# Column sums of the first modulation in pairs of channel tiles, with slab loads and weight loads on two issuing engines

## The chip, the cores and the metric

The kernel runs on one core of a Trainium2 chip. The metric is the device time of one execution in microseconds (us). Its engines run side by side, each with its own instruction list: TensorE (PE in the profile; PEld is its loading of weights), VectorE (DVE), ScalarE (ACT), GpSimd (POOL) and SyncE (SP). SP computes nothing: it issues transfers (DMAs) from device memory to the core. ScalarE can issue transfers too, in between its arithmetic.

## The reference

One layer of a diffusion backbone over 128 context tokens and 256 latent tokens, D_MODEL = 2048. What matters here is its beginning, for each of the two kinds of token:

```python
mod = jax.nn.silu(cond) @ lw['w_ada'] + lw['b_ada']
sh1, sc1, ga1, sh2, sc2, ga2 = [m[:, None, :] for m in jnp.split(mod, N_MOD, axis=-1)]
h = rmsnorm(x, lw['norm_pre_mix']) * (1.0 + sc1) + sh1
...
proj = h @ lw['w_in']      # columns: q | k | v | output gate | two low-rank factors | Fourier groups
```

After that come gated linear attention in both directions, a Fourier branch, the merge through sigmoid gates, an output projection and a SwiGLU feed-forward layer. All is in f32.

## The kernel before

All 384 tokens are kept transposed: 2048 channels are 16 channel tiles of 128 partitions, tokens run along the free axis. A product with a large weight is made in three passes: weight and activation are each split into a high part and a rest (`whi`/`wlo`, `A_hi`/`A_lo`, the latter being `hT[0]` and `hT[1]`), and high x high, high x rest and rest x high are added up. The high part is a copy on ScalarE (a cast), the rest a subtraction on VectorE.

The change is in the first stage, the first 140 us or so: a loop `for kb in range(KT)` over the 16 channel tiles. Tile `kb` of the normalised, modulated input h is made while tile `kb - 1` is multiplied into v, q and the low-rank factors. In an ordinary tile TensorE does, in this order:

- `gemv(kb)` (line 398): shift and scale of the tile's 128 channels, that is sums over all 2048 rows of `w_ada`, as 16 matmuls (32 records) that write 32 rows each into four row groups of the PSUM tile `pgm`. The weight slab of a tile (`slab`, 2 MB, in two halves of 1 MB) streams as the moving operand;
- a product into `px` (line 433 for one of two columns of q, or line 440, the low-rank factors, four tiles at a time, in tiles 6, 10 and 14);
- `vprod`, one of three passes of v (line 415): six matmuls of 512 columns;
- two transposes (line 515) of `ev`, to which ScalarE has copied the sums (line 509), back into `pgm`;
- the next `px` product, the second pass of v, possibly a third `px` product, and the third pass of v.

Behind the transposes VectorE forms the four row groups' sum `pm` (523), the modulation `mods` (526, 530) and the tile `scr` (532); ScalarE casts it to `A_hi` (302), VectorE subtracts for `A_lo` (303). Each `px` product is added to its accumulator by VectorE (`flush`, line 428) before `px` is written again. The splits of this tile's weights for v (`raw`: cast in 227, rest in 228) and q (`xraw`: cast in 363, rest in 364) are made in `split_w`; the subtractions are put off to the end of the tile (`lag`), behind `A_lo`. Tiles 1 and 2 (`wait`) have their sums later than the others, since slabs come late at the start.

The order on TensorE, ScalarE, VectorE and GpSimd is that in which the program is written (`manual_schedule`). SP, too, issues in the order written: in tile `kb` the two halves of slab `kb + 1` (`load_slab`, line 343), then the 512 KB of v's weights (`load`, line 199) and the 128 KB of q's (`load_w`, line 350) for tile `kb + 1`; after tile 4's also five small loads (`load_later`, lines 381 to 385). A load waits until its buffer is free: there are two of `raw`, two of `xraw`, and five half slabs. Each transfer signals its end on one of eight semaphores, which are dealt out in turn.

The same function `load` feeds all later stages; there SP issues its transfers.

Of the kernel before, what the change touches and what calls it, by code (L numbers as in the profile page):

```python
# [11 lines left out]
F32 = mybir.dt.float32  # L12
# [8 lines left out]
P = 128  # L21
D = 2048
KT = D // P
# [73 lines left out]
def tile_step(ctx: ExitStack, tc: tile.TileContext, a, o):  # L97
    nc = tc.nc
    PE, ACT, DVE, POOL, SP = nc.tensor, nc.scalar, nc.vector, nc.gpsimd, nc.sync
# [9 lines left out]
    spad = const.tile([P, KT, 32], F32, name="spad")  # L109
# [5 lines left out]
    ident = const.tile([P, P], F32, name="ident")  # L115
# [37 lines left out]
    for h in range(2):  # L153
        for n in range(8):
            src = a["w_in"][16 + 4 * h : 20 + 4 * h, n // 4, :, 256 * (n % 4) : 256 * (n % 4) + 256]
# [34 lines left out]
    srcs = iter(enumerate(srcs))  # L190
    raws, ready = [], []

    def load(raw=None):
        n, src = next(srcs, (0, None))
        if src is not None:
            if raw is None:
                raw = wp.tile([P, G], F32, tag="raw", name="raw", bufs=2)
            dst = raw if len(src.shape) == 2 else raw.rearrange("p (n x) -> p n x", n=src.shape[1])
            SP.dma_start(dst, src)
            raws.append((raw, n in folded))  # L200

    fold_in = []
# [42 lines left out]
    def take():  # L245
        return ready.pop(0)
# [54 lines left out]
    def split_act(hi, lo, src):  # L301
        ACT.copy(hi, src)
        DVE.tensor_sub(lo, src, hi.bitcast(F32))
# [31 lines left out]
    with ExitStack() as s:  # L335
        pa = s.enter_context(tc.tile_pool(name="pa", bufs=1))
        pb = s.enter_context(tc.tile_pool(name="pb", bufs=2))
        slabs = {}

        def load_slab(kb):  # L340
            slabs[kb] = [pb.tile([P, KT // 2, 256], F32, tag="slab", name="slab", bufs=5) for _ in range(2)]
            for n, sl in enumerate(slabs[kb]):
                SP.dma_start(sl, a["w_ada1"][kb, :, n * (KT // 2) : (n + 1) * (KT // 2), :])

        xraw = {}

        def load_w(kb):
            load()
            xraw[kb] = pb.tile([P, XU * P], F32, tag="xraw", name="xraw", bufs=2)
            SP.dma_start(xraw[kb], a["w_x"][kb])  # L350

        def split_w(kb, defer):

            hi, lo = (wp.tile([P, G], F32R, tag=n, name=n, bufs=4) for n in ("whi", "wlo"))
            hi, lo = hi[:, 0 : XU * P], lo[:, 0 : XU * P]
            raw = xraw.pop(kb)

            if kb == 0:
                ACT.copy(hi, raw)
                defer.append(lambda: DVE.tensor_sub(lo, raw, hi.bitcast(F32)))  # L360
            split(defer=defer)
            if kb:
                ACT.copy(hi, raw)
                defer.append(lambda: DVE.tensor_sub(lo, raw, hi.bitcast(F32)))
            return take(), (hi, lo)

        xn, xnt = halves("C")
        for q in range(4):
            SP.dma_start(
                xnt[q // 2][:, 4 * (q % 2) : 4 * (q % 2) + 4, :], a["xT"][:, 4 * q : 4 * q + 4, :],  # L370
            )
        load_slab(0)
        SP.dma_start(cols, a["b_ada"])
        SP.dma_start(norms, a["norms"])
        load_w(0)
        load_slab(1)
        load_w(1)
        wlr = pa.tile([P, KT, 32], F32, name="wlr")

# [8 lines left out]
        pv = [psm.tile([P, 512], F32, tag="mm", name="pv") for _ in range(3)]  # L388
        pv += [pss.tile([P, 512], F32, tag="side", name="pv") for _ in range(3)]
        pgm = pss.tile([P, 512], F32, tag="side", name="pgm")  # L390
        pgv, pmod = pgm[:, 0:256], pgm[:, 256:512]
        px = pss.tile([P, T], F32, tag="side", name="px")

        def gemv(kb, ks=range(KT)):
            slab = slabs[kb]
            for k in ks:
                q = 32 * (k % 4)
                PE.matmul(  # L398
                    pgv[q : q + 32, :], spad[:, k, :], slab[k // (KT // 2)][:, k % (KT // 2), :],
                    start=k < 4, stop=k >= KT - 4,  # L400
                )

        def passes(w):
            return ((0, w[0]), (0, w[1]), (1, w[0]))

        def vprod(kb, w, parts, ts=range(3)):
            js = passes(w)
            tg = [(t, g) for t in ts for g in range(2)]
            if kb < KT - 1:
                order = [(j, t, g) for j in parts for t, g in tg]  # L410
            else:
                order = [(j, t, g) for t, g in tg for j in parts]
            for j, t, g in order:
                x_, w_ = js[j]
                PE.matmul(  # L415
                    pv[2 * t + g], hT[x_][:, kb, t * P : (t + 1) * P], w_[:, g * 512 : (g + 1) * 512],
                    start=kb == 0 and j == 0, stop=kb == KT - 1 and j == 2,
                )
# [46 lines left out]
        DVE.tensor_scalar_add(bsc1[:, 0, :], cols[:, 1, :], 1.0)  # L465
        DVE.tensor_scalar_add(bsc1[:, 1, :], cols[:, 4, :], 1.0)
        gemv(0, range(KT // 2, KT))
        ev = pb.tile([P, 256], F32, tag="ev", name="ev")
        ACT.copy(ev, pgv)
        for t in range(3):  # L470
            PE.matmul(px[:, t * P : (t + 1) * P], r0[:, t : t + 1].to_broadcast([P, P]), ident, start=True, stop=True)
        rstd = pa.tile([P, T], F32, name="rstdA")
# [1 line left out]
        prev = None  # L474
        for kb in range(KT):
            if kb and kb + 1 < KT:
                load_slab(kb + 1)
                load_w(kb + 1)
                if kb == 4:
                    load_later()  # L480

            wait = kb in (1, 2)
            if kb and not wait:
                gemv(kb)
            todo = []
            if kb > 4 and kb % 4 == 2:
                todo.append(lrprod(kb - 6))
            if kb:
                todo += [xprod(u, kb - 1, prev[1]) for u in range(XU)]
            todo += [None] * (4 - len(todo))  # L490
            flushes = [t[1] if t else lambda: None for t in todo]

            def pe_x(n):
                if todo[n]:
                    todo[n][0]()

            if wait:
                vprod(kb - 1, prev[0], (0,))
            pe_x(0)
            hf = scr[:, kb % 8, :]  # L500

            xr = hf if kb else qs[0]
            DVE.tensor_mul(xr, xn(kb), rstd if kb else px)
            flushes[0]()
            if wait:
                gemv(kb)
            if kb:
                ev = pb.tile([P, 256], F32, tag="ev", name="ev")
                ACT.copy(ev, pgv)
            lag = []  # L510
            new = split_w(kb, lag)
            if kb:
                vprod(kb - 1, prev[0], (1 if wait else 0,))
            for m in range(2):
                PE.transpose(pmod[:, m * P : (m + 1) * P], ev[:, m * P : (m + 1) * P], ident)
            if kb == 0:

                for _ in range(6):
                    PE.matmul(pv[5][:, 0:P], ones, ones, start=True, stop=True)
            pe_x(1)  # L520

            pm = pb.tile([P, 2, 2], F32, tag="pm", name="pm", bufs=2)
            DVE.tensor_reduce(
                pm, pmod.rearrange("p (m q r) -> p m r q", m=2, q=4)[:, :, 0:2, :], axis=mybir.AxisListType.X, op=ALU.add,
            )
            DVE.tensor_scalar(
                mods[:, 1, kb, :], pm[:, 1, :], bsc1[:, 0, kb : kb + 1], norms[:, 0, kb : kb + 1],
                op0=ALU.add, op1=ALU.mult,
            )
            DVE.tensor_scalar_add(mods[:, 0, kb, :], pm[:, 0, :], cols[:, 0, kb : kb + 1])  # L530
            for lo, hi, c in segs:
                DVE.tensor_scalar(
                    hf[:, lo:hi], xr[:, lo:hi], mods[:, 1, kb, c : c + 1], mods[:, 0, kb, c : c + 1],
                    op0=ALU.mult, op1=ALU.add,
                )
                if kb == 0:
                    ACT.activation(
                        hT[0][:, kb, lo:hi], xr[:, lo:hi], AF.Identity,
                        bias=mods[:, 0, kb, c : c + 1], scale=mods[:, 1, kb, c : c + 1],
                    )  # L540
            flushes[1]()
            if kb:
                split_act(hT[0][:, kb, :], hT[1][:, kb, :], hf)
            else:
                ACT.copy(rstd, px)
                DVE.tensor_sub(hT[1][:, kb, :], hf, hT[0][:, kb, :].bitcast(F32))
            if kb:
                if not wait:
                    vprod(kb - 1, prev[0], (1,))
                pe_x(2)  # L550
                flushes[2]()
            for sub in lag:
                sub()
            if kb:
                vprod(kb - 1, prev[0], (2,))
                pe_x(3)
                flushes[3]()
            prev = new
# [72 lines left out]
    with ExitStack() as s:  # L631
# [9 lines left out]
        for c in range(2):  # L641
            src = a["a2"][:, 512 * c : 512 * c + 512]
# [192 lines left out]
        for c in range(2):  # L835

            dst = a2.rearrange("p (h d j) -> p d h j", d=2, j=P)[:, c]
            raw, up = (x.rearrange("p (h j) -> p h j", j=P) for x in (raw3[1 + c][0:98, 0:512], part[0:98]))
# [264 lines left out]
    mg32, _ = halves("B")  # L1103
    x1, x1t = halves("C")
    with ExitStack() as s:
# [49 lines left out]
        for i in range(KT):  # L1155
            p = psm.tile([P, T], F32, tag="mm", name="pmm")
            for g in range(2):
                n = 2 * i + g - 2 * KT
# [381 lines left out]
        n = 0  # L1540
# [85 lines left out]
        for kind, c, i in steps:  # L1626
# [8 lines left out]
            if kind == "D":  # L1635
                w = grab2()
                n, kh = i // 2, i % 2
                if kh == 0:
# [3 lines left out]
                    pool, tag = (pss, "side") if done % 2 or (c, n) == (NFC - 2, 3) else (psm, "mm")  # L1642
# [52 lines left out]
        n = d_order[-1]  # L1695
# [145 lines left out]
```

## Time and profile before

| | |
|---|---|
| median of 3 runs | 1956.16 us (1956.04 to 1958.14) |
| profiled execution | 1956.59 us, its span 1954.8 us |
| busy, share of the span | PE 99%, PEld 87%, DVE 83%, ACT 46%, POOL 2% |
| granted TensorE clock | 0.999 |
| moved by DMA | 380.11 MB, mean 194 GB/s |
| loop over the 16 channel tiles | from about 18 to 137 us |

A profile row gives, for a group of instructions, the start and duration in us, the engine, the line of the kernel, the operation, out<-in by the program's names, and in brackets how long the engine stood idle before it and what ended that. The chain of work that ended last follows back from the last instruction, at each step to what released it; its rows are start, duration and the work. In the table of stretches a row has the stretch, its length, the busy time and number of instructions of each engine, the clock, the share of the DMA engines' time and the rate. Ends of matmuls are modelled, so starts are the better measure on TensorE.

### The profile page before, as it was taken

To read this page: it belongs to the slowest core of one execution; us is meant where nothing else is said; L and a number is where in the kernel's file an instruction comes from. 1 tells how busy PE (TensorE), PEld (TensorE's weight loads), DVE (VectorE), ACT (ScalarE), POOL (GpSimd) and SP (SyncE) were. 2 spreads that over 40 slices of the span, in tenths; PEclk is the share of its full clock that TensorE was granted. 3 is DMA by queue.
4 is the path that set the end of the run, shared out by engine and by line. 5 is a ranking of instruction groups with operands and counts; after the bars stand their busy time and mean duration, and the time that the engine had idled before them with its cause. 6 is when DMAs were issued, how large, how long until landed. Compare 5 with 4: busy or idle time off the path is not lost.

```text
span 1954.8 us, 27236 instructions
## 1 busy us (share of the span) xinstructions
PE 1937.6 (99%) x10430; PEld 1705.3 (87%) x10430; DVE 1632.0 (83%) x2097; ACT 905.4 (46%) x1265; POOL 32.7 (2%) x45
## 2 busy tenths in 40 slices
PE   8999999999999999999999999999999999999998
PEld 5779999999899999999988888888888888888886
DVE  5679888878777797977789998999898999887875
ACT  4233554544336654446454444444444444444444
POOL 0000000000000000004000000000000000000001
PEclk9999999999999999999999999999999999999999
DMA  9968777767765786655355535463636363626243
GB/s 390 388 248 275 231 247 239 232 218 244 239 199 177 230 266 214 223 193 212 94 154 164 171 125 181 136 199 110 199 124 205 94 217 104 209 67 194 76 161 130
DMA packets 195994, 380.11 MB, mean 194 GB/s; under 512 B 14096, under 2 KB 121300, under 8 KB 191512
## 3 DMA queue, kind: packets, MB, share of 16 engines
q1 hardware_dynamic: 195720, 377.98, 58.9%
q8 instruction: 82, 1.34, 0.3%
q14 instruction: 48, 0.39, 0.1%
q10 hardware_dynamic: 144, 0.39, 0.1%
HBM read 361.55 MB, written 16.78 MB: 194 GB/s over the span
## 4 chain that ended last, share of the span: by engine, by line
PE 92%; issue 3%; DMA 3%; DVE 1%; ACT 1%; POOL 0%; SPq 0%; POOLq 0%; ACTq 0%; DVEq 0%
PE pgu L273 31%; PE pmm L261 30%; PE pdn L273 16%; PE pfo L273 3%; PE pv L415 3%; PE pgm L398 1%; PE pmm L1311 1%; PE pf L1055 1%; PE px L433 1%; DMA slab<-in_w_ada 1%; PE ptr L1603 1%; DMA xraw<-in_w_x 1%; PE po L664 1%; PE pf L1056 0%; DMA raw<-in_w_br_gla 0%
## 5 line engine op out<-in xcount | busy, mean ns | idle before, releaser
L261 PE MATMUL pmm<-A_hi,whi 128*128 128x384 f32 x1072 | 361.2, 337 | 0.0
L261 PE MATMUL pmm<-A_hi,wlo 128*128 128x384 f32 x1072 | 358.6, 335 | 0.0
L261 PE MATMUL pmm<-A_lo,whi 128*128 128x384 f32 x1072 | 358.5, 334 | 0.0
L1458 ACT CAST whi<-u 128x1024 fp32r<-128x1024 f32 x200 | 210.5, 1053 | 274.9 <-DVE u L1442 87.1
L1458 ACT CAST whi<-raw 128x1024 fp32r<-128x1024 f32 x175 | 184.2, 1053 | 210.6 <-DMA raw<-in_w_g 72.4
L227 ACT CAST whi<-raw 128x1024 fp32r<-128x1024 f32 x181 | 189.4, 1051 | 190.8 <-DMA raw<-in_w_gate 63.6
L228 DVE TENSOR_TENSOR wlo<-raw,whi 128x1024 fp32r<-128x1024 f32 x179 | 217.8, 1220 | 69.0 <-ACT whi L227 67.3
L1469 DVE TENSOR_TENSOR wlo<-u,whi 128x1024 fp32r<-128x1024 f32 x200 | 243.8, 1219 | 28.7 <-ACT whi L1458 17.5
L273 PE MATMUL pgu<-whi,A_hi 128*128 128x512 f32 x640 | 250.0, 391 | 0.0
L273 PE MATMUL pgu<-whi,A_lo 128*128 128x512 f32 x640 | 249.3, 389 | 0.0
L1469 DVE TENSOR_TENSOR wlo<-raw,whi 128x1024 fp32r<-128x1024 f32 x175 | 213.2, 1218 | 33.0 <-ACT whi L1458 19.6
L591 DVE SCALAR_TENSOR_TENSOR adacc<-adaw,spad,adacc 128x1024 f32<-128x1024 f32 x180 | 222.7, 1278 | 1.5 <-DMA adaw<-in_w_ada 1.2
L261 PEld LDWEIGHTS pmm<-A_hi,whi 128*128 128x128 f32 x1072 | 201.2, 188 | 2.6 <-issue 1.4
L261 PEld LDWEIGHTS pmm<-A_lo,whi 128*128 128x128 f32 x1072 | 201.3, 188 | 0.2
L261 PEld LDWEIGHTS pmm<-A_hi,wlo 128*128 128x128 f32 x1072 | 201.2, 188 | 0.0
L273 PE MATMUL pdn<-whi,hid_hi 128*128 128x512 f32 x480 | 186.9, 389 | 0.0
L273 PE MATMUL pdn<-whi,hid_lo 128*128 128x512 f32 x480 | 186.8, 389 | 0.0
L273 PE MATMUL pgu<-wlo,A_hi 128*128 128x512 f32 x640 | 184.2, 389 | 0.0
L273 PEld LDWEIGHTS pgu<-whi,A_hi 128*128 128x128 f32 x640 | 120.1, 188 | 26.0 <-issue 0.8
L273 PEld LDWEIGHTS pgu<-wlo,A_hi 128*128 128x128 f32 x640 | 120.2, 188 | 25.3
L273 PEld LDWEIGHTS pgu<-whi,A_lo 128*128 128x128 f32 x640 | 120.2, 188 | 25.0
L273 PE MATMUL pgu<-whi,S 128*128 128x512 f32 x480 | 131.1, 395 | 0.0
(379 smaller groups left out, 2900.6 us busy)
## 6 DMA issues: line engine op xcount, KB each, us to landing
adaw<-in_w_ada SPq DMA_DIRECT2D x96, 512.0 KB, 3.9
raw<-in_w_d SPq DMA_DIRECT2D x88, 512.0 KB, 4.5
slab<-in_w_ada SPq DMA_DIRECT2D x32, 1024.0 KB, 9.8
raw<-in_w_gate SPq DMA_DIRECT2D x64, 512.0 KB, 4.7
raw<-in_w_g SPq DMA_DIRECT2D x48, 512.0 KB, 3.9
raw<-in_w_u SPq DMA_DIRECT2D x48, 512.0 KB, 3.7
raw<-in_w_in SPq DMA_DIRECT2D x44, 512.0 KB, 4.3
u<-in_w_u SPq DMA_DIRECT2D x40, 512.0 KB, 4.7
```

What stands on the lines that cost most here:

```text
L227: ACT.copy(hi, raw)
L228: sub = lambda: eng.tensor_sub(lo, raw, hi.bitcast(F32))
L261: PE.matmul(dst, w[wi][:, k * n + n0 : k * n + n0 + P], x[xi][:, k0 + k, :], start=first and k == 0 and j == 0, stop=last and k == kts - 1 ...
L273: PE.matmul(dst, stat[x_][m], mov(w[w_], m), start=first and w_ == m == x_ == 0, stop=last and w_ == m == 1,)
L398: PE.matmul(pgv[q : q + 32, :], spad[:, k, :], slab[k // (KT // 2)][:, k % (KT // 2), :], start=k < 4, stop=k >= KT - 4,)
L415: PE.matmul(pv[2 * t + g], hT[x_][:, kb, t * P : (t + 1) * P], w_[:, g * 512 : (g + 1) * 512], start=kb == 0 and j == 0, stop=kb == KT - 1 ...
L433: PE.matmul(px, w_[:, u * P : (u + 1) * P], hT[x_][:, kb, :], start=j == 0, stop=j == 2)
L591: DVE.scalar_tensor_tensor(acc[:, c, :], w, spad[:, k, c : c + 1], acc[:, c, :], op0=ALU.mult, op1=ALU.add,)
L664: PE.matmul(dst, w[wi], x[xi], start=first and j == 0, stop=last and j == 2)
L1055: PE.matmul(pf[:, 0 : 2 * HT], w[0][:, c], x[k], start=k == 0, stop=False)
L1458: ACT.copy(hi, src)
L1469: DVE.tensor_sub(lo, src, hi.bitcast(F32))
```

## The change

From tile 8 on the sums are made for two tiles at once: at the even tile, `gemv(kb)` and `gemv(kb + 1)` stand back to back, into columns 0 to 255 and 256 to 511 of `pgm`. One copy brings all 512 columns to `ev` (now one buffer of 512 columns, before two of 256). Each tile of the pair still has its own two transposes, into its own half of `pgm`. An odd tile thus has no sums, and the order of its products is that of the tiles called `wait`: the first v pass at the head, the second ahead of the transposes, the third at the end.

Slabs are now loaded in a sequence of their own (`next_slab`) with six half buffers: as before to slab 4; in tile 3 also slab 5, so that from tile 4 on slab `kb + 2` is issued in tile `kb`. SP issues the slabs and the small loads alone from tile 4 on. The weights of v and q for tiles 5 to 15 are issued by ScalarE, in tile `kb` for tile `kb + 1`, behind that tile's two casts. After the loop `load` is SP's again.

```diff
-    def load(raw=None):
+    def load(raw=None, eng=SP):
...
-            SP.dma_start(dst, src)
+            eng.dma_start(dst, src)
...
-            slabs[kb] = [pb.tile([P, KT // 2, 256], F32, tag="slab", name="slab", bufs=5) for _ in range(2)]
+            slabs[kb] = [pb.tile([P, KT // 2, 256], F32, tag="slab", name="slab", bufs=6) for _ in range(2)]
...
-        def load_w(kb):
-            load()
+        def load_w(kb, eng=SP):
+            load(eng=eng)
             xraw[kb] = pb.tile([P, XU * P], F32, tag="xraw", name="xraw", bufs=2)
-            SP.dma_start(xraw[kb], a["w_x"][kb])
+            eng.dma_start(xraw[kb], a["w_x"][kb])
...
-        pgv, pmod = pgm[:, 0:256], pgm[:, 256:512]
...
-        def gemv(kb, ks=range(KT)):
+        def gemv(kb, ks=range(KT), at=0):
...
-                    pgv[q : q + 32, :], spad[:, k, :], slab[k // (KT // 2)][:, k % (KT // 2), :],
+                    pgm[q : q + 32, at : at + 256], spad[:, k, :], slab[k // (KT // 2)][:, k % (KT // 2), :],
...
             if kb and kb + 1 < KT:
-                load_slab(kb + 1)
-                load_w(kb + 1)
+                next_slab()
+                if kb < 4:
+                    load_w(kb + 1)
+                if kb == 3:
+                    next_slab()
                 if kb == 4:
                     load_later()
 
             wait = kb in (1, 2)
-            if kb and not wait:
+
+            pair = kb >= 8
+
+            early = wait or pair and kb % 2 == 1
+            if pair and kb % 2 == 0:
+                for n in range(2):
+                    gemv(kb + n, at=256 * n)
+            elif kb and not wait and not pair:
                 gemv(kb)
...
-            if wait:
+            if early:
                 vprod(kb - 1, prev[0], (0,))
...
-            if kb:
-                ev = pb.tile([P, 256], F32, tag="ev", name="ev")
-                ACT.copy(ev, pgv)
+            at = 256 * (kb % 2) if pair else 0
+            if kb and at == 0:
+                n = 512 if pair else 256
+                ev = pb.tile([P, 512], F32, tag="ev", name="ev", bufs=1)
+                ACT.copy(ev[:, 0:n], pgm[:, 0:n])
+            pmod = pgm[:, at : at + 256] if pair else pgm[:, 256:512]
             lag = []
             new = split_w(kb, lag)
+            if 4 <= kb < KT - 1:
+                load_w(kb + 1, ACT)
             if kb:
-                vprod(kb - 1, prev[0], (1 if wait else 0,))
+                vprod(kb - 1, prev[0], (1 if early else 0,))
             for m in range(2):
-                PE.transpose(pmod[:, m * P : (m + 1) * P], ev[:, m * P : (m + 1) * P], ident)
+                PE.transpose(pmod[:, m * P : (m + 1) * P], ev[:, at + m * P : at + (m + 1) * P], ident)
...
-                if not wait:
+                if not early:
                     vprod(kb - 1, prev[0], (1,))
```

More of the change, by code (lines that the diff above doesn't have):

```diff
@@ L371, in tile_step, with next_slab @@
             )
-        load_slab(0)
+        slab_order = iter(range(KT))
+        def next_slab():
+            kb = next(slab_order, None)
+            if kb is not None:
+                load_slab(kb)
+        next_slab()
         SP.dma_start(cols, a["b_ada"])
@@ L375, in tile_step @@
         load_w(0)
-        load_slab(1)
+        next_slab()
         load_w(1)
@@ L467, in tile_step @@
         gemv(0, range(KT // 2, KT))
-        ev = pb.tile([P, 256], F32, tag="ev", name="ev")
-        ACT.copy(ev, pgv)
+        ev = pb.tile([P, 512], F32, tag="ev", name="ev", bufs=1)
+        ACT.copy(ev[:, 0:256], pgm[:, 0:256])
         for t in range(3):
@@ L476, in tile_step @@
             if kb and kb + 1 < KT:
-                load_slab(kb + 1)
-                load_w(kb + 1)
+                next_slab()
+                if kb < 4:
+                    load_w(kb + 1)
+                if kb == 3:
+                    next_slab()
                 if kb == 4:
@@ L506, in tile_step @@
                 gemv(kb)
-            if kb:
-                ev = pb.tile([P, 256], F32, tag="ev", name="ev")
-                ACT.copy(ev, pgv)
+            at = 256 * (kb % 2) if pair else 0
+            if kb and at == 0:
+                n = 512 if pair else 256
+                ev = pb.tile([P, 512], F32, tag="ev", name="ev", bufs=1)
+                ACT.copy(ev[:, 0:n], pgm[:, 0:n])
+            pmod = pgm[:, at : at + 256] if pair else pgm[:, 256:512]
             lag = []
             new = split_w(kb, lag)
+            if 4 <= kb < KT - 1:
+                load_w(kb + 1, ACT)
             if kb:
-                vprod(kb - 1, prev[0], (1 if wait else 0,))
+                vprod(kb - 1, prev[0], (1 if early else 0,))
             for m in range(2):
-                PE.transpose(pmod[:, m * P : (m + 1) * P], ev[:, m * P : (m + 1) * P], ident)
+                PE.transpose(pmod[:, m * P : (m + 1) * P], ev[:, at + m * P : at + (m + 1) * P], ident)
             if kb == 0:
```

## The prediction

> **What bounds the kernel now.** I read the table of stretches first, to see which engine is full in the first 145 us (the only part that the change touches), then the chain in order of time, to see what one channel tile is made of.
>
> ```profile
> 20.00:40.00 20.00, 19.34 (x156) 12.54 (x155) 12.75 (x29) 6.48 (x13) 0.00 (x0) 1.00 1.02 412
> 40.00:60.00 20.00, 20.00 (x152) 14.71 (x152) 13.31 (x32) 5.39 (x11) 0.00 (x0) 1.00 0.96 366
> 100.00:120.00 20.00, 20.00 (x150) 14.95 (x143) 11.98 (x30) 6.42 (x12) 0.00 (x0) 1.00 0.94 347
> 120.00:140.00 20.00, 19.96 (x148) 13.76 (x146) 13.71 (x29) 6.40 (x11) 1.03 (x3) 1.00 0.41 147
> ```
>
> The columns are the stretch, its length, busy time of PE, PEld, DVE, ACT and POOL, PE's granted clock, the DMA engines' busy share and GB/s. PE misses 0.66 us between 20 and 40 us and nothing worth naming afterwards, at full clock. The DMA engines are nearly as full: what they move at a share of 1.02 is 412 GB/s. So PE's own time sets the end of this stage, and the loads stand close behind it.
>
> ```profile
> 25.39 12.34 DMA slab<-in_w_ada
> ...
> 37.78 1.07 PE pgm L398 x16
> ...
> 44.46 1.86 PE pgm L398 x32
> ...
> 98.70 1.86 PE pgm L398 x32
> 100.57 0.72 PE px L433 x3
> 101.29 1.38 PE pv L415 x6
> 102.67 0.22 PE pgm L515 x2
> 102.89 0.52 PE px L433 x3
> 103.41 2.76 PE pv L415 x12
> ...
> 122.97 0.65 PE px L440 x8
> 123.61 1.59 PE pv L415 x6
> ```
>
> The rows from 98.70 are tile 11: sums over K (1.86), first q product (0.72), a third of v (1.38), two transposes (0.22), second q product (0.52), the rest of v (2.76); together 7.46 us, and tile 12's sums follow at once. The same q product takes 0.72 behind the sums and 0.52 behind the transposes: coming back from matmuls that write 32 rows to ones that write 128 costs 0.20 us. Where the low-rank product (L440, also 32 rows) stands in between, the 0.2 moves to the v product behind it (1.59 against 1.38). Going the other way shows no cost: twelve v matmuls take 2.76, twice 1.38. The two rows at 25.39 and 37.78 are the one place where PE waits for a load: the second half of tile 3's slab.
>
> **The change, part by part.**
>
> *Pairs.* The sums of tiles 9, 11, 13 and 15 move directly behind those of 8, 10, 12 and 14. No matmul is added or taken away; four returns to 128 rows go: 4 x 0.20 = 0.80 us. Bounds: nothing, if the second sum of a pair leaves a gap of its own; 4 x 0.28 = 1.12, from the half sums, which cost 2 x 1.07 = 2.14 apart and 1.86 in one piece. I take 0.80, which is the same switch seen directly. The eviction to ev becomes one of 512 columns instead of two of 256; ScalarE is busy 6 of 20 us, so it is hidden. The single ev buffer is free long before: its reader, the transpose of the odd tile, comes a whole even-tile sum ahead.
>
> *The odd tiles' new order.* Without sums at its head, an odd tile starts with v products that need the even tile's A_hi, and then a q product that needs its xraw split. These rows of the timeline are tile 11's:
>
> ```profile
> 101.91 0.41 ACT L363 CAST whi<-xraw 128x256 fp32r<-128x256 f32 x1
> ...
> 102.51 0.38 PE L515 MATMUL pgm<-ident,ev 128*128 128x128 f32 x2
> ...
> 104.37 0.51 ACT L302 CAST A_hi<-scr 128x384 fp32r<-128x384 f32 x1 [2.05 <-DVE scr L532]
> ...
> 106.53 0.42 DVE L364 TENSOR_TENSOR wlo<-xraw,whi 128x256 fp32r<-128x256 f32 x1
> ...
> 109.37 0.41 ACT L363 CAST whi<-xraw 128x256 fp32r<-128x256 f32 x1
> ```
>
> From the transposes' start (102.51) A_hi is ready after 2.37 us and the low part of xraw after 4.44. PE still has 0.22 + 0.52 + 2.76 = 3.50 of even-tile work behind that start, so A_hi is hidden by 1.1; with the odd tile's first v product (1.38) PE comes to the q product after 4.88: hidden by 0.4. Cost 0.
>
> *The end of the loop.* Tile 15 is odd: a third of v goes ahead of its transposes, so 1.38 us less stands between them and the last v products, which need tile 15's own split.
>
> ```profile
> 136.24 1.22 DVE L228 TENSOR_TENSOR wlo<-raw,whi 128x1024 fp32r<-128x1024 f32 x1
> ...
> 138.07 0.39 PE L415 MATMUL pv<-wlo,A_hi 128*128 128x512 f32 x1
> ```
>
> wlo is ready at 137.46, its first reader starts at 138.07. Against the transposes that reader now comes at 138.07 - 1.38 = 136.69, so PE waits 0.77 there: a stall that did not exist. Bounds 0 and 1.38; I take 0.77. What waits next is DVE itself, in order.
>
> *Six half slabs instead of five.* Tile 3's second half no longer waits for the buffer of tile 1's first half. It can win at most the 0.66 that PE misses in that stretch, and nothing if the DMA engines, at a share of 1.02 there, merely carry the same bytes in the same order. I take 0.2, near the lower end, because of that share. It cannot lose: nothing is put ahead of it.
>
> *The weights on ScalarE's queue, tiles 5 to 15.* Two issues a tile leave SP and stand on ScalarE behind the two casts and ahead of A_hi.
>
> ```profile
> 1948.95 0.41 ACTq L1762 DMA_DIRECT2D out_yT<-x1b  x1
> ```
>
> ```profile
> adaw<-in_w_ada SPq DMA_DIRECT2D x96, 512.0 KB, 3.9
> ```
>
> ScalarE's one issue in the trace takes 0.41, so 0.82 a tile, inside the 2.05 that it idles ahead of A_hi: hidden. They wait for the buffers of two tiles earlier, which DVE has released by then. The new risk is time to land. xraw is issued at 101.91 + 0.41 + 0.41 = 102.73 and cast at 109.37: 6.6 us, where SP used to issue a whole tile ahead. The row nearest to a lone load is adaw's: 512 KB land in 3.9 us, and xraw's 128 KB behind it add 0.3 at 412 GB/s; so 4.2 when nothing competes. The other end is what loads of raw took on the one shared queue:
>
> ```profile
> DMA to landing us min/median/max: 4.6/8.6/12.2
> ```
>
> Those stood behind slabs in one order; on a queue of their own they need not. A late cast is at first free: A_hi has 2.05 - 0.82 = 1.2 us to give, and behind it the next tile's q product leaves another 1.2 (its low part is ready at 106.95, and is read 0.2 into the product that starts 1.86 after the next sums at 106.17, that is 108.2). I take a landing near 6, cost 0.
>
> *Slabs alone on SP.* SP no longer stops for raw's buffers, and slabs run up to three tiles ahead; they were not late after 38 us. Pairs need slab 9 only 1.86 us after slab 8, but it is issued when tile 6 gives up its buffers, two tiles earlier, some 15 us. Cost 0.
>
> **The sum**: 1956.59 (the profiled execution; its span is 1954.8) - 0.80 - 0.2 + 0.77 = 1956.4. The median of the runs shown is 0.43 below that execution, so 1955.9; I say 1956.0. A measurement of this kernel tells about 0.2% (3.9 us) from no change, so this is no change.
>
> **Rivals.**
>
> *The weights land late (slower).* For it: the DMA engines are full to about 100 us in any case, and now slabs always stand in SP's queue beside ScalarE's loads. The sizes of the pieces matter:
>
> ```profile
> DMA packets 11186, 48.65 MB, mean 347 GB/s; under 512 B 2128, under 2 KB 4176, under 8 KB 7078
> ```
>
> In the first 140 us 4108 packets are of 8 KB or more, which is 32 half slabs of 128 rows of 8 KB; raw has rows of 4 KB, xraw of 1 KB. An engine moves 412/16 = 25.8 GB/s, so 0.32, 0.16 and 0.04 us a row. If the two queues take turns row by row, each engine's eight rows of raw take 8 x 0.48 = 3.8 and those of xraw 8 x 0.36 = 2.9; with the 2.6 that a lone load takes beyond its bytes (3.9 - 1.3) and the 0.4 between the issues, xraw lands 8.9 us after its issue, 2.3 over the 6.6. ScalarE's loop (land, cast, issue) is then the longer one: lateness grows by 2.3 a tile, 2.4 of it are free, one tile in four is 1 us longer. PE's wait is about 2 in tile 7, 1 in tile 8, and about 1 in each pair after that, as the DMA engines catch up meanwhile: some 3 to 9 us, 1959 to 1965. It decides from a landing of about 7 us on. Against it: ScalarE's own queue spares them the slabs queued ahead, and a PE that waits lets slabs drain. [...] Chance 0.22.
>
> *ScalarE is held by the turn of the semaphores (slower).*
>
> ```profile
> 39.59 1.43 SPq L343 DMA_DIRECT2D slab<-in_w_ada  x2
> ...
> 47.23 0.43 SPq L384 DMA_DIRECT2D gnorm<-in_gnorm  x1
> 48.96 0.33 SPq L385 DMA_DIRECT2D selr<-in_consts  x1
> 51.50 1.65 SPq L343 DMA_DIRECT2D slab<-in_w_ada  x2
> ```
>
> From 39.59 to 47.23 SP issues eight loads (two half slabs, raw, xraw and four small ones); the ninth waits to 48.96 and the tenth to 51.50, and nothing they need is late: a load waits until the eighth before it has landed, here slab 5's halves. If raw 5, issued in tile 4, gets the turn behind slab 5's second half and xraw 5 that behind slab 6's first, ScalarE stands until about 51.5 + 1.05 MB/412 GB/s = 54.0, and A_hi of tile 4, due at 44.46 + 5.7 = 50.1, and the next eviction behind it, come 4.3 late. With 1.2 to give at the q product PE waits 3.1: 1959.1. It depends on the order in which the turns are dealt out, which the trace doesn't show; with both loads dealt ahead of the five small ones they wait only for slab 4, long landed. Chance 0.07.
>
> *Faster.* All the idle time that PE has from 20 to 140 us is 0.8, and the pairs win 1.12 at most: 1956.16 - 1.8 = 1954.4 is the floor without the stall at the end. More than 0.2% would need PE's own matmuls to shorten, for which no row speaks. Chance 0.05, of which little is beyond 0.2%.
>
> **How the numbers follow.** No change as summed: 0.66. The range takes in the floor, 1954.2 with the spread of the runs, and most of the late loads: up to 1963, which leaves out about 0.1 above and 0.04 below. Slower by over 0.2% (beyond 1960.1) takes most of the late loads, a part of the held ScalarE and what I haven't thought of: 0.26. Faster 0.04, within 0.70.
>
> **What would show it.** Right: in the chain, sums of 3.7 us at every second tile from 8 on, and odd tiles whose q products both take 0.52; PE idle about 0.8 ahead of the last v products with DVE's wlo as releaser; casts of raw and xraw on ScalarE that follow without a wait for DMA. Wrong: ScalarE's casts of xraw waiting for in_w_x from tile 6 on, and px or pv waiting for A_hi or wlo (the first rival); ScalarE idle ahead of an issue in tile 4 (the second); the first q product of an odd tile still at 0.72 (no gain from the pairs).

## The result: 12 us slower, and the profile after

The changed kernel takes 1968.55 us (median of 4 runs, 1968.26 to 1970.01) against 1956.72 for the one before on the same chip: a ratio of 1.0061, with a 95% interval from 1.0049 to 1.0072. The forecast was 1956.0 with a range from 1954.2 to 1963.0, so it missed on the slow side. The profiled execution took 1968.79 us, its span is 1966.5.

Nearly all of it is lost in the stage of the change. The next stage's first product (`pmm`) starts at 143.23 us before and at 154.27 after, 11.0 us of the 11.7 between the spans. Where in the stage, TensorE's timeline of the changed kernel shows (start, duration, engine, line, operation; in brackets the idle time ahead and what ended it):

```profile
67.81 1.07 PE L404 MATMUL pgm<-slab,spad 128*32 128x256 f32 x16
70.08 1.07 PE L404 MATMUL pgm<-slab,spad 128*32 128x256 f32 x16 [1.21 <-DMA slab<-in_w_ada]
...
76.69 1.93 PE L404 MATMUL pgm<-slab,spad 128*32 128x256 f32 x32
80.02 1.07 PE L404 MATMUL pgm<-slab,spad 128*32 128x256 f32 x16 [1.41 <-DMA slab<-in_w_ada]
83.34 1.93 PE L404 MATMUL pgm<-slab,spad 128*32 128x256 f32 x16 [2.24 <-DMA slab<-in_w_ada]
85.20 0.69 PE L439 MATMUL px<-A_hi,whi 128*128 128x384 f32 x1
...
86.33 2.76 PE L421 MATMUL pv<-whi,A_hi 128*128 128x512 f32 x6
88.89 0.59 PE L536 MATMUL pgm<-ident,ev 128*128 128x128 f32 x2
89.17 0.48 PE L439 MATMUL px<-A_hi,whi 128*128 128x384 f32 x1
...
98.10 3.66 PE L404 MATMUL pgm<-slab,spad 128*32 128x256 f32 x64
...
113.69 3.66 PE L404 MATMUL pgm<-slab,spad 128*32 128x256 f32 x64
...
131.54 3.66 PE L404 MATMUL pgm<-slab,spad 128*32 128x256 f32 x64
```

Up to 67.81 nothing has happened (the kernel before starts the same sums at 67.78). Then the second half of slab 7 is late, and both halves of slab 9, which the pair of tiles 8 and 9 needs. The best ruler for the rest is a version of the changed kernel with the weights back on SyncE (the second experiment below), which has the same order on TensorE and no loss:

```profile
75.19 4.01 PE L404 MATMUL pgm<-slab,spad 128*32 128x256 f32 x64
...
79.14 0.45 PE L439 MATMUL px<-A_hi,whi 128*128 128x384 f32 x1
...
79.78 1.55 PE L421 MATMUL pv<-whi,A_hi 128*128 128x512 f32 x6
81.17 0.38 PE L536 MATMUL pgm<-ident,ev 128*128 128x128 f32 x2
81.31 0.43 PE L439 MATMUL px<-A_hi,whi 128*128 128x384 f32 x1
...
90.18 3.66 PE L404 MATMUL pgm<-slab,spad 128*32 128x256 f32 x64
...
105.77 3.66 PE L404 MATMUL pgm<-slab,spad 128*32 128x256 f32 x64
...
120.36 3.66 PE L404 MATMUL pgm<-slab,spad 128*32 128x256 f32 x64
```

Line against line, the changed kernel is behind by 1.5 us at tile 8's sums (76.69 against 75.19), 6.1 behind slab 9 (85.20 against 79.14), 7.9 at the next q product (89.17 against 81.31), 7.9 at tiles 10 and 12, and 11.2 at tile 14. So there are three parts: 6.1 us up to the end of slab 9's sums, of which 4.9 are the three waits for slabs (1.21, 1.41 and 2.24); 1.8 between two rows with no wait in between; and 3.3 in tiles 12 and 13.

The 1.8 is the clock. From the table of stretches of the changed kernel (length, busy time of PE, PEld, DVE, ACT, POOL, granted clock, DMA share, GB/s):

```profile
82.00:84.00 2.00, 0.66 (x8) 0.40 (x12) 0.00 (x0) 0.00 (x0) 0.00 (x0) 0.62 1.02 411
84.00:86.00 2.00, 2.00 (x14) 1.00 (x7) 0.00 (x0) 0.61 (x2) 0.00 (x0) 0.50 1.04 434
86.00:88.00 2.00, 2.00 (x6) 1.66 (x6) 0.56 (x1) 1.23 (x2) 0.00 (x0) 0.50 1.01 418
88.00:90.00 2.00, 2.00 (x9) 1.66 (x8) 0.38 (x3) 0.00 (x0) 0.00 (x0) 0.67 1.03 424
```

While TensorE waited for slab 9 the granted clock fell to half, and it stayed there from about 82.5 to about 89.3 us (0.62 and 0.67 are means of stretches that are in part at 0.50 and in part at 1.00), though the last half slab had come at 83.34: six v matmuls take 2.56 us from start to start (86.33 to 88.89) where the ruler takes 1.39 (79.78 to 81.17). The same fall has a part in the 6.1 us: the sums of the last half slab take 1.86 us (83.34 to 85.20), where a quarter of the ruler's 3.95 for four half slabs (75.19 to 79.14) is 1.0. In all the clock takes some 2.7 us. Ahead of the fall at 82.5 TensorE was not idle throughout: it waited 1.41 us, worked for 1.07 and had waited some 1.4 of the 2.24. In the version with early weights on ScalarE (below) the clock stayed at 1.00 behind waits of 1.17 and 2.13 us. What sets off the fall no run here shows.

The last part, tiles 12 and 13, is in the chain that ended last (start, duration, what):

```profile
103.19 11.64 DMA xraw<-in_w_x
...
115.00 7.84 DMA raw<-in_w_v
...
122.86 1.05 ACT whi L227
...
123.92 0.40 ACT whi L363
...
124.84 0.52 ACT A_hi L302
...
131.61 3.59 PE pgm L404 x64
...
147.82 1.15 DVE wlo L228
...
149.01 1.43 PE pv L421 x5
```

A load of 128 KB takes 11.64 us from issue to landing, the next one of 512 KB 7.84, and behind them come the casts, A_hi, and TensorE. The lower rows are the stall at the end of the loop: v's last products wait for `wlo`.

What SyncE and ScalarE waited for in the first 150 us of the changed kernel (engine and line, what for: total us, times, longest):

```profile
SPq L343 <- DMA raw<-in_w_v: 20.2, 4, 8.1
...
SPq L343 <- DMA xraw<-in_w_x: 7.3, 2, 5.3
SPq L389 <- DMA raw<-in_w_v: 5.4, 1, 5.4
```

```profile
ACT whi L227 <- DMA raw<-in_w_v: 10.1, 4, 4.9
ACT whi L363 <- DMA xraw<-in_w_x: 8.8, 5, 3.2
```

The second pair of lines is the expected trouble: casts that wait for their loads. The first is the one that matters most at tiles 7 to 9: SyncE, which issues slabs and small loads alone, stands still until ScalarE's weights have landed. A slab has nothing to do with raw; what joins them is the turn of the eight semaphores. The trace's records of the issues name the semaphore of each transfer. The second half of slab 9, for instance, has the one that raw 7 had before (each line: the transfer's place in the turn, issuing engine, tile, and who had its semaphore eight places earlier):

```
36  SP      coef     <- ScalarE  raw 5
38  SP      gnorm    <- ScalarE  xraw 5
42  SP      slab 7b  <- ScalarE  xraw 6
49  SP      slab 9b  <- ScalarE  raw 7
51  SP      slab 10b <- ScalarE  xraw 7
```

The second halves of slabs 7 and 9 are issued at 63.9 and 70.6 us, where SyncE issues them at 57.0 and 64.1 when it has the weights too. In the kernel before, SyncE waited ahead of a slab for a weight once, for 0.9 us. In the trace everything behind an issue that waits stands on SyncE too: `coef` waits 5.4 us and is issued at 54.43, `gnorm` waits another 2.0, and slab 7 behind them is issued at 58.18.

### The profile page after: what moved, and what is told of

The parts are those of the page before. It is cut to its first block, busy times and chain, and to the rows that moved or that the text cites. A ratio compares the mean times of both kernels' runs of the same rounds, so it can differ in the third digit from the quotient of the medians.

```text
span 1966.5 us, 27208 instructions
## 1 busy us (share of the span) xinstructions
PE 1940.3 (99%) x10430; PEld 1707.2 (87%) x10430; DVE 1632.1 (83%) x2097; ACT 906.6 (46%) x1261; POOL 32.7 (2%) x45
## 4 chain that ended last, share of the span: by engine, by line
PE 89%; issue 2%; DMA 1%; DVE 1%; ACT 1%; POOL 0%; POOLq 0%; ACTq 0%; SPq 0%; DVEq 0%
PE pmm L261 32%; PE pgu L273 30%; PE pdn L273 16%; PE pfo L273 3%; PE pf L1076 1%; PE pmm L1332 1%; PE pv L421 1%; PE ptr L1624 1%; DMA xraw<-in_w_x 1%; PE pf L1077 1%; PE po L685 1%; DMA raw<-in_w_v 0%; PE dl L685 0%; PE pp L931 0%; DMA x1b<-x_d 0%
## 6 DMA issues: line engine op xcount, KB each, us to landing
slab<-in_w_ada SPq DMA_DIRECT2D x32, 1024.0 KB, 11.8
```

## The experiments

Two theories to begin with. Theory A: ScalarE's weights land late, and through the shared semaphores they make SyncE's slabs late. Theory B: the DMA engines, full to 110 us (a share of 0.90 to 1.02 before), can't have slab 9 there only 1.9 us after slab 8, whoever issues it; the pairs are at fault. All ratios are against runs of the kernel before on the same chip (medians 1956.7 to 1957.0).

**No pairs.** Every tile forms its own sums, as before the change; the rest is as changed.

```diff
-            pair = kb >= 8
+            pair = False
```

> The changed kernel without the pairs: one tile's sums at a time to the end, everything about the loads as changed. The changed kernel is 11.8 us above the kernel before; in its trace PE loses about 7.8 us in tiles 7 to 9 (waits for slabs and the low clock that follows), 3 in tiles 12 and 13 (weights late), 0.8 at the end. Theory A (the two issuing engines are chained by the eight semaphores, so slabs 7 to 9 are issued late and weights land late): slab 7 still late by 1.4 us, slab 9 needed a tile later and no longer late, weights still late: 2 to 6 us above before. Theory B (bytes: by tile 8 the DMA engines cannot have brought slab 9 whatever the order): the loads as such cost nothing, 0 to 1.4 above before. Late weights as the main cause: 4 or more above.

Measured: 1969.01 us, 1.0060 [1.0045, 1.0075]. The loss is all there without pairs, so theory B falls; of the forecasts only the one for late weights, 4 us or more, holds. The loss only moves: ScalarE's casts wait 28.9 us for raw (7 times, longest 8.1) and 12.0 for xraw.

**Weights on SyncE.** The same order on TensorE, but SyncE issues the weights, in the place where ScalarE did.

```diff
-                load_w(kb + 1, ACT)
+                load_w(kb + 1, SP)
```

> The changed kernel with pairs and six half slabs, but the weights of tiles 5 to 15 issued by SyncE again, at the place in the program where ScalarE had them. Theory A (late issue through the semaphores across two engines, late weights on their own queue): both go, the time is within 1 us of before. Theory B (bytes): tile 8 still waits for slab 9, 3 to 6 us above before, low clock included.

Measured: 1957.19 us, 1.0000 [0.9991, 1.0009]. Who issues the weights is the whole loss; pairs, six half slabs and slabs issued early cost nothing. TensorE doesn't wait for slab 9; its one wait for a slab is 0.2 us at 37.7 us, where it also stood before the change. A cast that waits is no loss in itself: ScalarE's casts wait 13.2 us for raw here too, 4.2 at the longest.

**Weights on GpSimd.**

```diff
-                load_w(kb + 1, ACT)
+                load_w(kb + 1, POOL)
```

> The changed kernel with the weights of tiles 5 to 15 issued by GpSimd, whose transfers signal on other semaphores than those of SyncE and ScalarE; still a queue of their own. Theory A in its first half (slabs late because SyncE waits for the landing of ScalarE's weights): slabs 7 to 9 are issued as soon as their buffers are free, the hole in the DMA traffic at 55 to 65 us closes, some 6 of the 7.8 us of tiles 7 to 9 go; what is left, 3 to 6 us above before, is late weights. Theory B: tile 8 waits for slab 9 as in the changed kernel, 10 to 12 us above before. If the weights' own queue beside the slabs were all of it: still 10 or more.

Measured: 1957.45 us, 1.0000 [0.9991, 1.0009]. This is a miss for both theories, which gave 3 to 6 us and 10 to 12 us above the kernel before. So a second issuing engine is not in itself slow. By the records of the issues GpSimd's transfers have semaphores of their own (another eight), and ahead of slabs SyncE waits for no weight:

```profile
SPq L343 <- PE pgm L404: 39.6, 12, 12.6
```

That is only the buffer: SyncE is ahead of TensorE. But a second thing differs. GpSimd has nothing else to do, and issues a load as soon as VectorE has freed the buffer (in tile 8 at 76.25 us), where ScalarE comes to it only with its casts (in tile 8 at 85.54, behind the late slab). The landing is not shorter: raw takes 8.2 us in the median here, 5.3 in the changed kernel. It is hidden.

**Small loads on GpSimd.** The five loads of `load_later` leave SyncE; they fill the place in the queue at 50 to 60 us in which the changed kernel's DMA engines run dry (175 GB/s from 55 to 60 us).

```diff
-            SP.dma_start(wlr, a["w_lr"])
+            POOL.dma_start(wlr, a["w_lr"])
... the other four likewise
```

> The changed kernel with only the five small loads (w_lr, coefficients, b_gate, gnorm, selector) issued by GpSimd instead of SyncE, so that SyncE goes from slab 6 to slab 7 without them and they take no turn of the eight semaphores. Theory A: slabs 7 and 8 are issued about 50 us instead of 58 to 65, most of the 7.8 us go, late weights stay: 3 to 7 us above before. Theory B: no change from the changed kernel, 10 to 12 above.

Measured: 1970.47 us, 1.0067 [1.0050, 1.0084], a miss for both theories. The hole is gone (416 GB/s from 50 to 60 us) and TensorE waits 0.4 us for slabs, but the time stays: ScalarE's casts now wait 37.9 us for raw. Slabs in time are not enough; the weights alone can make up the whole loss.

So from here on three theories. *Turn*: the shared semaphores hold SyncE. *Late place*: ScalarE issues the weights behind its casts of the tile, and issue, landing and cast in a circle last longer than a tile. *Queue*: ScalarE's queue lands later than others.

**ScalarE, but early.** The weights are issued by ScalarE at the head of the tile, ahead of its copy and casts.

```diff
                 next_slab()
-                if kb < 4:
-                    load_w(kb + 1)
+                load_w(kb + 1, SP if kb < 4 else ACT)
...
-            if 4 <= kb < KT - 1:
-                load_w(kb + 1, ACT)
```

> Three theories for the twelve microseconds. Turn: the eight semaphores go round SyncE and ScalarE together, so a slab of SyncE waits until a weight of ScalarE has landed. Late place: ScalarE issues the weights only behind its own casts of the tile, some 3.5 us after the buffer is free, and issue, landing and cast together last longer than a tile, so the loop sets the pace. Queue: what ScalarE's queue issues lands later than what the other queues issue. Here the weights stay on ScalarE but are issued at the head of the tile, ahead of its copy and casts. By the late place 1956 to 1959 us; by the turn 1963 to 1970, since SyncE's slabs still wait for landings of ScalarE's weights; by the queue 1966 to 1970, unchanged.

Measured: 1963.16 us (1960.50 to 1966.06), 1.0031 [1.0019, 1.0043]: half the loss is gone. On the same queue ScalarE's casts now wait 3.0 us in all for v's and q's weights, where they waited 18.9, and raw lands after 8.0 us in the median, against 8.2 from GpSimd at its own pace; *queue* falls. What is left is SyncE's waits and TensorE's waits for slabs:

```profile
SPq L343 <- DMA raw<-in_w_v: 26.9, 5, 10.6
...
SPq L343 <- DMA xraw<-in_w_x: 10.6, 5, 2.4
```

```profile
PE pgm L404 <- DMA slab<-in_w_ada: 3.9, 4, 2.1
```

The clock has a part in it as well. This trace is of the shortest of the six executions (1960.50 us), whose mean granted clock is 0.999; the three longest, 1964.33 to 1966.06 us, have 0.997.

**Three buffers.** ScalarE issues in its late place, but two tiles ahead, into three buffers of raw and xraw (`lracc` doubles as the second square sum to make room).

```diff
+            third = pb.tile([P, G], F32, tag="raw3", name="raw", bufs=1) if kb % 3 == 2 else None
-            load(eng=eng)
-            xraw[kb] = pb.tile([P, XU * P], F32, tag="xraw", name="xraw", bufs=2)
+            load(third, eng=eng)
+            xraw[kb] = pb.tile([P, XU * P], F32, tag="xraw", name="xraw", bufs=3)
...
-            if 4 <= kb < KT - 1:
-                load_w(kb + 1, ACT)
+            if kb == 4:
+                load_w(5, ACT)
+            if 4 <= kb < KT - 2:
+                load_w(kb + 2, ACT)
```

> Three buffers each for raw and xraw; ScalarE issues the weights two tiles ahead, in the same place behind its casts (the second square sum and the low-rank accumulator share a buffer to make room). A landing of 8 to 12 us then has two tiles' time. By the late place 1956 to 1959 us, casts waiting below 3 us in all. By the turn 1962 to 1970: SyncE still stands behind landings of the weights, and slabs stay late at the seventh to ninth tile. By the queue 1956 to 1960 as well, with landings above 10 us.

Measured: 1964.43 us, 1.0035 [1.0022, 1.0048]. The same half goes in another way. Casts wait 2.9 us in all for these weights, TensorE 4.7 for slabs, and the clock falls to 0.64 between 80 and 85 us.

**GpSimd, but late.** GpSimd issues the weights, held back by a one-column copy of what ScalarE has just cast. No turn is shared, and ScalarE's queue is not used.

```diff
...
-                load_w(kb + 1, ACT)
+                POOL.tensor_copy(late, new[1][0][:, 0:1].bitcast(F32))
+                load_w(kb + 1, POOL)
```

> GpSimd issues the weights, but held back to about ScalarE's place by a one-column copy of what ScalarE has just cast. No transfer of the weights then takes a semaphore of SyncE's slabs, and ScalarE's queue isn't used. By the late place 1960 to 1969 us, with ScalarE's casts waiting 15 us or more for raw and xraw; by the turn and by the queue 1956.5 to 1958.5, as with GpSimd at its own pace (1957.45).

Measured: 1969.04 us, 1.0062 [1.0047, 1.0077], 11.6 more than GpSimd at its own pace. TensorE waits 0.3 us for slabs, ScalarE 47.5 for raw. This is the late place alone, on a queue that did no harm when used early:

```profile
59.12 0.54 POOL L199 DMA_DIRECT2D raw<-in_w_v  x1 [0.34 <-DMA bgate<-in_b_gate]
...
69.75 0.53 POOL L199 DMA_DIRECT2D raw<-in_w_v  x1 [0.34 <-issue]
...
81.40 0.54 POOL L199 DMA_DIRECT2D raw<-in_w_v  x1 [0.34 <-issue]
```

One circle lasts 10.6 and 11.7 us, where a tile has 7.5. (The copy and GpSimd's own issues, 0.53 to 0.54 us for one of raw, lengthen it by an estimated 1 us or so, so the size isn't ScalarE's.)

**Slabs on GpSimd, two failures.** To free the slabs from the turn they were issued by GpSimd: first from slab 6 on, with the five small loads, and the weights late on ScalarE; then from slab 8 on, with the weights early on ScalarE.

```diff
-                SP.dma_start(sl, a["w_ada1"]...
+                (SP if kb < 6 else POOL).dma_start(sl, a["w_ada1"]...     # second version: kb < 8
...
```

> Slabs from the seventh (kb 6) on and the five small loads are issued by GpSimd, the weights by ScalarE in the place of the changed kernel, so no transfer of the one takes a semaphore that the other waits for. By the turn 1956 to 1959 us, with ScalarE's casts waiting less than 6 us in all for the weights. By the late place 1962 to 1970: the slabs are in time, but ScalarE's casts still wait 20 us or more for raw and xraw. By the queue the same 1962 to 1970.

> ScalarE issues the weights at the head of the tile, and GpSimd issues the slabs from kb 8 on, so these slabs share no semaphore turn with ScalarE's weights; slabs up to kb 7 and the small loads stay on SyncE. With the early weights alone the kernel was at 1963.16 us, with halves of slab 9 landing late at tile 8. If the turn is what makes those slabs late: 1956.5 to 1959 us, and waits of TensorE for slabs below 1.5 us in all. If it is only that two queues share the DMA engines: 1962 to 1965 us with the same waits as there, some 4 us.

Measured: 1969.81 us, 1.0066 [1.0049, 1.0082], and 1967.72 us, 1.0051 [1.0037, 1.0064]. The first lies where the late place was expected, with casts that wait 27.2 us in all. But neither tells of the turn, since slabs overtook each other. In the first, GpSimd issued slab 6 and the small loads at 38 to 42 us, ahead of SyncE's slab 5, and tile 4's raw was cast at 50.42 instead of 46.7. In the second, GpSimd had issued slab 8 at 53.38, while SyncE, still held by the turn, issued the last half of slab 7 only at 64.39; TensorE got it at 75.50 and waited for slabs 5.5 us in all, so the forecast for the second missed by 9 us.

**The four corners.** The repair: GpSimd issues all slabs from 6 on, slab 6 only when ScalarE has cast tile 4's q weights. No slab from 6 on shares a turn with a weight, and none overtakes. The weights are issued by ScalarE, once early, once late.

```diff
-                SP.dma_start(sl, a["w_ada1"]...
+                (SP if kb < 6 else POOL).dma_start(sl, a["w_ada1"]...
...
-                next_slab()
-                if kb < 4:                                  # kept in the late version
-                    load_w(kb + 1)
+                if kb != 4:
+                    next_slab()
+                load_w(kb + 1, SP if kb < 4 else ACT)       # early version alone
...
             new = split_w(kb, lag)
+            if kb == 4:
+                POOL.tensor_copy(late, new[1][0][:, 0:1].bitcast(F32))
+                next_slab()
-            if 4 <= kb < KT - 1:                            # kept in the late version
-                load_w(kb + 1, ACT)
```

> All slabs from kb 6 on are issued by GpSimd, slab 6 held back until ScalarE has cast tile 4's q weights (so that it doesn't run ahead of slab 5), and ScalarE issues the weights at the head of the tile. No slab from kb 6 on shares a turn with a weight. With the same early weights and the slabs on SyncE the kernel was at 1963.16 us, SyncE waiting 27 us for raw and 11 for xraw ahead of slabs. If the turn makes the slabs late: 1956.5 to 1959.5 us, waits of TensorE for slabs below 1.5 us. If two busy queues side by side make them late: 1962 to 1966 us, with some 4 us of such waits and a clock below 1 behind them.

> The same slabs on GpSimd, but ScalarE issues the weights behind its casts, in the place of the changed kernel. By the late place 1963 to 1970 us, with ScalarE's casts waiting 20 us or more for raw and xraw, although no slab shares a turn with them. If the turn were all of it: 1956.5 to 1959.5 us.

Measured: early 1958.48 us, 1.0007 [0.9998, 1.0016]; late 1965.07 us, 1.0043 [1.0031, 1.0056]. With the two kernels that have slabs on SyncE this makes a square:

| | weights early on ScalarE | weights late on ScalarE | late place costs |
|---|---|---|---|
| slabs on SyncE, turn shared | 1963.16 | 1968.55 (the change) | 5.4 |
| slabs on GpSimd, no turn shared | 1958.48 | 1965.07 | 6.6 |
| the turn costs | 4.7 | 3.5 | |

Both causes are real, each about half (6.0 and 4.1 us in the mean of the square), and with both gone the kernel is within what can be told from no change. The intervals of the four ratios reach 1.8 to 2.5 us to either side, so a difference in the square is uncertain by some 3 us (an estimate that takes the four as independent). Slabs on GpSimd stand on another queue as well, but that is not what brings them in time: with slabs left on SyncE and weights on GpSimd, which shares no turn either, TensorE waits 0.7 us for slabs when the weights are issued early and 0.3 when they are late. In the early version TensorE waits 1.0 us for slabs where the same weights with a shared turn made it 3.9:

```profile
PE pgm L405 <- DMA slab<-in_w_ada: 1.0, 3, 0.5
```

And the late version shows the circle on ScalarE without any turn (ACT is its arithmetic, ACTq its issues):

```profile
66.14 0.34 ACTq L199 DMA_DIRECT2D raw<-in_w_v  x1
66.59 0.37 ACTq L351 DMA_DIRECT2D xraw<-in_w_x  x1
...
75.07 1.05 ACT L227 CAST whi<-raw 128x1024 fp32r<-128x1024 f32 x1 [4.64 <-DMA raw<-in_w_v]
77.94 0.41 ACT L364 CAST whi<-xraw 128x256 fp32r<-128x256 f32 x1 [1.82 <-DMA xraw<-in_w_x]
78.02 0.34 ACTq L199 DMA_DIRECT2D raw<-in_w_v  x1
78.47 0.38 ACTq L351 DMA_DIRECT2D xraw<-in_w_x  x1
```

Issue at 66.14, landing by 75.07 (8.9 us), xraw by 77.94 (11.4), next issue at 78.02: 11.9 us a round against 7.5 for a tile. The early version issues its loads in tile 8 at 76.02, ahead of the copy at 79.87, and no cast waits more than 1.8 us for its load.

**Three pairs, weights on SyncE**, the best that the runs point to: tiles 14 and 15 form their sums apart, so that the stall at the end of the loop goes.

```diff
-            pair = kb >= 8
+            pair = 8 <= kb < 14
...
-                load_w(kb + 1, ACT)
+                load_w(kb + 1, SP)
```

> Weights on SyncE in the place where the changed kernel has them on ScalarE, and pairs for tiles 8 to 13 only, so that tiles 14 and 15 form their sums one at a time. With the weights on SyncE and all four pairs the kernel stood at 1957.19 us, and its trace showed the saving of the pairs (0.8), a wait of 0.2 for a slab and the stall at the end of the loop (0.8). Without the stall and with three pairs: 0.2 less for the pair given up, 0.8 less stall, so 1956.4 to 1956.8 us, faster than before by up to 0.6 us, which is less than 0.05%.

Measured: 1955.94 us, 0.9995 [0.9986, 1.0004]. The median is below the forecast (1956.4 to 1956.8) and 0.9 us below the kernel before, but the interval holds 1, so it isn't shown to beat it. Its trace has `pmm` start at 142.64 us, against 143.23 before and 143.05 with four pairs.

## Why the prediction was wrong, step by step

- *Pairs*, −0.80: right. In the chain 64 matmuls of sums take 3.59 us, and the q products of odd tiles 0.52 to 0.53. The version with three pairs and no end stall starts `pmm` 0.59 us earlier, about three times 0.20.
- *The odd tiles' new order*, 0: right where the loads are in time. With the weights on SyncE, TensorE waits neither for A_hi nor for xraw's low part in tiles 9, 11 and 13.
- *The end of the loop*, +0.77: right in place and releaser (`wlo` at 147.82 to 148.96, v at 149.01). The profile puts the wait at 0.5 us; taking the stall away together with one pair won 0.41 (143.05 to 142.64), which makes 0.6 for the stall.
- *Six half slabs*, −0.2: the lower end held, nothing. Tile 7's sums start at 67.78 before, 67.81 after and 67.73 with the weights on SyncE.

The sum of these four steps was −0.23 us, and where SyncE has the weights `pmm` starts 0.18 earlier than before. What failed are the two steps that moved the loads.

- *The weights on ScalarE's queue*, 0, with a landing "near 6": the step that failed first. The rows of the changed kernel for tile 9:

```profile
85.54 0.33 ACTq L199 DMA_DIRECT2D raw<-in_w_v  x1
...
85.99 0.37 ACTq L350 DMA_DIRECT2D xraw<-in_w_x  x1
...
93.54 1.05 ACT L227 CAST whi<-raw 128x1024 fp32r<-128x1024 f32 x1 [2.07 <-DMA raw<-in_w_v]
97.75 0.41 ACT L363 CAST whi<-xraw 128x256 fp32r<-128x256 f32 x1 [3.16 <-DMA xraw<-in_w_x]
97.83 0.33 ACTq L199 DMA_DIRECT2D raw<-in_w_v  x1
```

  raw lands after 8.0 us, xraw after 11.8. The prediction had both ends (4.2 for a lone load, 12.2 from the shared queue) and took the lower half, because a queue of its own "need not" stand behind slabs. It also had the working of the circle in a rival: "ScalarE's loop (land, cast, issue) is then the longer one". That rival was right in its mechanism and in its sign, with a landing of 8.9; without the turn it predicted 1959 to 1965, and the late place without the turn gives 1965.07, at the upper end. The row that should have decided is the DMA share: at 1.02, no load is a lone one. The price of the step, 5.4 to 6.6 us, is not in the landing but in the moved place: an issue that stands behind casts which wait for the issue before it can't run ahead.

  The rival's picture of two queues taking turns row by row gave 3.8 us for raw and 2.9 for xraw behind it. In the late version of the square xraw's cast starts 2.9 us behind raw's (75.07 and 77.94). The 2.9 agrees, but the whole landing of 8.9 is 2.5 longer than the 6.4 that this working gives for raw. The trace's records of single rows (a row is what goes to one partition), which no view prints, show both. Of the changed kernel's raw 9, issued at 85.54, the 128 rows move within 3.80 us, and in these 128 rows of slabs move too, at 0.16 and 0.31 us a row: one for one, as the rival had assumed. The term that it had too small is the time up to the first row, 3.45 us here and 1.0 for the loads of tiles 13 to 15, beside which no slab row moves. Why raw 9 waited so long for its first row no run here shows.
- *Slabs alone on SP*, 0: the second step that failed, 3.5 to 4.7 us. "SP no longer stops for raw's buffers" was true, but it stops for raw's landing instead, by the turn. The prediction knew the turn and looked at the wrong engine: its rival has ScalarE held behind slabs in tile 4 (chance 0.07). Raw 5 and xraw 5 have the places 28 and 30 in the turn, ahead of the five small loads, and ScalarE issues them at 46.63 and 47.10 us without a wait. The opposite direction, SyncE held behind ScalarE's weights, was not worked out, although it follows from the same rule, and it is the worse one: what SyncE issues is what TensorE needs next. The reason given, that slab 9 is issued two tiles earlier, was read from the buffers alone.
- The clock, not in the prediction at all: some 2.7 us in the profiled execution.
- The floor under *Faster* adds 0.8 and 1.12 to 1.8, where they make 1.9; nothing hangs on it.
- What would show it: the sign given for the first rival (casts of xraw that wait, from tile 5 on, px and pv that wait for A_hi or `wlo`) came, and the one for the second (ScalarE idle ahead of an issue in tile 4) did not.

That the two causes don't quite add (5.4 and 6.6 for the late place, 4.7 and 3.5 for the turn) is no finding: the 1.2 us lie within the noise of the square. Open is the clock's part in each: in the changed kernel it fell during TensorE's wait for slab 9, it differs between executions of one kernel (a mean of 0.997 to 0.999 with early weights on ScalarE), and was not taken away in any run.

## What to carry to other kernels

When a load moves to another engine, ask what stands ahead of it in that engine's program, not only whether the engine has time: an issue behind an instruction that waits for the issue before closes a circle of issue, landing and use, and the circle must be shorter than the tile (here rounds of 10.6 to 12.3 us against 7.5). Issue at the point where the buffer comes free, or have one buffer more (here casts then waited 3.0 and 2.9 us in all for the weights, against 18.9). And when two engines issue, look whom the semaphores join: where they are dealt out in one round, a transfer of one engine waits for the landing of an unrelated one of the other, and everything behind it on its engine waits too (here SyncE stood ahead of slabs 20.2 us for raw and 7.3 for xraw).

## What was not expected of the hardware

- A load of 128 KB (rows of 1 KB) on ScalarE's queue took 11.8 us to land where the one of 512 KB issued 0.45 us before it took 8.0, on DMA engines at a mean share of 1.01 from 85.99 to 97.75 us.
- During the second of two waits of 1.41 and 2.24 us within 4.7 us TensorE's clock fell to 0.50, for 6.8 us (82.5 to 89.3); six v matmuls in it took 2.56 us from start to start, against 1.39 with the weights on SyncE. In the version with early weights on ScalarE waits of 1.17 and 2.13 us at the same place left the clock at 1.00 in the profiled execution; other executions of the same kernel, with a mean clock of 0.997, were up to 5.6 us longer.
- On ScalarE's queue raw 5, 8, 9, 11 and 12 had their first row moved 3.0 to 3.6 us after their issue, beside rows of slabs; raw 6 and 13 to 15, beside which no slab row moved, 1.0 us after it. But raw 7 had it after 1.9 us and raw 10 after 1.0, with slab rows beside them.
